# Modulation on VectorE, and the two halves of the square sums joined on GpSimd, in an 8-core encoder step

## The chip, the cores and the metric

The kernel runs on the 8 cores of one Trainium2 chip. The metric is the device time of the slowest core in microseconds (us), and smaller is better. Most executions of one kernel agree within 0.3%. In some executions the cores of one die (cores 0 to 3, or 4 to 7), in one execution of the kernel before those of both (0.851 to 0.898, 3065.08 us), show a lower granted TensorE clock, and the time is some per cent longer or more. Such executions are on record for 11 of the 20 kernels here, the kernel before among them; what brings them on is not shown. They are called slow here, and no conclusion rests on them.

TensorE is PE in the profile, its weight load PEld, VectorE DVE, ScalarE ACT, GpSimd POOL, SyncE SP. "L655" is line 655 of the kernel in question; line numbers differ between the kernels, because each has its own text. One helper line issues every matmul, so that line alone does not tell one matmul from another; tile names and shapes do.

## The reference, cut to what matters

There are four layers, prompts of 4 x 4096 rows and 16 sample streams of 16 rows. Every layer has two RMSNorms, each with shift, scale and gate from a conditioning vector `c`.

```python
D_MODEL, SEQ, DEPTH = 1024, 4096, 4

def rms_norm(x, g):
    xf = x.astype(jnp.float32)
    y = xf * lax.rsqrt(jnp.mean(xf * xf, axis=-1, keepdims=True) + EPS)
    return (y * g.astype(jnp.float32)).astype(x.dtype)

def trunk_layer(x, c, hist, pos0, ...):                   # cut
    mod = jnp.dot(jax.nn.silu(c), w_ada) + b_ada          # (B, 6*D): six vectors per sequence
    sh_m, sc_m, gt_m, sh_f, sc_f, gt_f = [m[:, None, :] for m in jnp.split(mod, N_MOD, axis=-1)]
    h = rms_norm(x, g_mix) * (1 + sc_m) + sh_m
    z = jnp.dot(h, w_in)
    p = z[..., :POOL_WIDTH]
    u = jax.nn.gelu(z[..., POOL_WIDTH:POOL_WIDTH + GMLP_WIDTH])
    v = layer_norm(jax.nn.gelu(z[..., POOL_WIDTH + GMLP_WIDTH:]), ln_g, ln_b)
    ...                                                   # pooling mixer, spatial gating: cut
    x = x + gt_m * mix
    h = rms_norm(x, g_ffn) * (1 + sc_f) + sh_f
    f = jnp.dot(jax.nn.silu(jnp.dot(h, w_gate)) * jnp.dot(h, w_up), w_down)
    x = x + gt_f * f
    return x, new_hist, v
```

## The kernel before

The kernel is a Python program that lists some thousands of operations, orders them with a list scheduler of its own, and then emits one instruction stream per engine. The scheduler places each operation by a cost that is written beside it, in us. An operation may name two engines (`flex`: VectorE or ScalarE), and then the scheduler chooses. Two programs are made: even cores take the first half of a prompt and 64 sample rows, odd cores the second half. Each core picks its program at run time (the "role branch").

The activations lie transposed in SBUF: 128 partitions times 8 blocks (`KC`) make the 1024 features, and rows run along the free dimension. The mean of squares over the features is then a sum over partitions, which a matmul with a constant matrix `meanb` (every element 1/1024) does. For 256 rows:

```python
def stats(src, n, Rsrc, rs, ro, Rrs, lead, add=ADD):      # ADD = 4
    kk, bk = (4 if n > 128 or add < ADD else KC), bank()
    for k0 in range(0, KC, kk):                           # two halves of four blocks each
        q, ks = r_sq.new(), kk // add
        p = r_sp.new() if add > 1 else q
        ...
        flex(... out=sv(), in0=src[:, k0:k0+kk, :], in1=src[:, k0:k0+kk, :], op=ALU.mult), 0.065 + kk*n/960,
             ... activation(out=sv(), in_=src[:, k0:k0+kk, :], func=AF.Square), 0.067 + kk*n/1200, ...)
        m = kk
        while m > ks:                                     # 4 blocks -> 2 -> 1, the last one in bf16
            m //= 2
            dve(... out=pv() if m == ks else sv(0, m), in0=sv(0, m), in1=sv(m, 2*m), op=ALU.add), ...)
        pe(mms(None, lambda ...: [(B(bk)[:, 0:n], meanb[:, :], pv()[:, k, :],
                                   k0 + k == 0, k0 + kk == KC and k == ks - 1) for k in range(ks)]), ...)
    act(... AF.Ln ...)                                    # Ln, then Exp with scale -0.5: the rsqrt
    act(... AF.Exp, scale=-0.5 ...)
```

So each half of the features has its own averaging matmul, and the two accumulate in one PSUM bank. The modulation is 12 groups per layer, each of 32 matmuls with 1 column (odd cores) or 5 (even cores):

```python
def mods(l, g, w):
    bk, m = bank(), l % 2
    def specs():
        wv = V(w, 128, (4, KC * 128))
        return [(B(bk)[:, NV*c:NV*c + NV], wv[:, c, 128*k:128*k + 128], scT[:, k, 0:NV], k == 0, k == KC - 1)
                for c in range(4) for k in range(KC)]
    pe(mms(None, specs), 32 * 0.026, [Rscb, w.res[0]], [bk.res[0]])
    dve(... tensor_tensor(out=modT[...], in0=B(bk)[...], in1=b_adaT[...], op=ALU.add) ...)
```

The sample rows' p and v projections use 64 of the 128 output rows, and come one after the other:

```python
def rows_(self, i, o, nb, w):                             # cut: nb is 64 for sample rows
    pe(mms(None, lambda: [(B(bk)[0:nb, :], V(h, 128, (KC, N))[:, k, o:o + nb], V(w, 128, (KC, 512))[:, k, :],
                           k == 0, k == KC - 1) for k in range(KC)]), ...)
```

Last, `fills`: where the scheduler expects PE to wait long, it has PE run `meanb` x `meanb` matmuls that nobody reads, meant to keep the clock up; whether they do was not tested. They count as busy in the profile (244 of them on core 7, 18.5 us), although they are waiting.

## Time and profile before

The median of the first 6 runs was 2671.88 us (2669.75 to 3100.27, the longest ones slow). The page of the profiled execution (core 7, its slowest), its busy line and three of its rows of 40 slices (each digit is the busy share in tenths; PEclk is the granted clock):

```profile
PE 2616.3 (98%) x17898; PEld 1569.8 (59%) x17898; DVE 1632.1 (61%) x3073; ACT 946.9 (35%) x1603; POOL 181.0 (7%) x311
...
PE   5999999999999999999999999999999999999997
...
PEclk8999999999999999999999999999999999999999
...
PE 93%; DVE 2%; issue 2%; ACT 1%; DMA 1%; ACTq 0%; POOL 0%; another core or an unknown queue 0%; DVEq 0%; POOLq 0%
```

The last line is the chain of waits that ended last. PE is nearly always busy and makes 93% of that chain; only the first slice and the last have room. VectorE and ScalarE are far from full. Two groups of matmuls are what the change is after (name of the tiles, shapes, count, busy us, mean ns, then the idle time before them and what ended it):

```profile
L647 PE MATMUL bank<-heap,meanb 128*128 128x256 bf16 (+2 forms) x174 | 38.3, 263 | 22.0 <-DVE heap L790 18.9
...
L647 PE MATMUL bank<-scT,heap 128*128 128x1 bf16 x1536 | 45.3, 163 | 8.2 <-ACT heap L1198 8.0
```

The first are averaging matmuls, the second modulation. The mean of 163 ns is a pipelined duration. From start to next start a modulation matmul takes about 26 ns, one of 256 columns 109 ns and one of 512 columns 216 ns. The cores view shows that odd cores are the slowest by about 9 us, and that the clock is nearly full:

```profile
core 0: 2662.1 us, clock 0.995
core 1: 2667.6 us, clock 0.994
...
core 6: 2660.9 us, clock 0.993
core 7: 2670.6 us, clock 0.993
```

The windows view of core 7 says where PE idles (columns: window, its length, then busy time and instructions of PE, PEld, DVE, ACT, POOL, the granted clock, the DMA share and GB/s):

```profile
0.00:67.00 67.00, 39.07 (x469) 31.27 (x470) 24.72 (x54) 25.44 (x41) 16.69 (x31) 0.90 0.99 203
67.00:215.00 148.00, 142.06 (x1308) 101.08 (x1306) 133.92 (x296) 103.74 (x176) 18.34 (x37) 0.97 0.61 123
215.00:1500.00 1285.00, 1284.03 (x8489) 746.16 (x8488) 783.84 (x1448) 424.00 (x720) 65.83 (x136) 1.00 0.30 56
1500.00:2630.00 1130.00, 1126.05 (x7304) 669.89 (x7303) 664.14 (x1222) 370.23 (x623) 69.81 (x103) 1.00 0.25 50
2630.00:2671.00 41.00, 25.10 (x336) 21.42 (x333) 25.49 (x57) 23.52 (x47) 10.29 (x5) 0.88 0.27 101
```

Between 215 and 2630 us, PE idles 0.97 + 3.95 = 4.9 us in all. The rest is the start, where data has to arrive (DMA share 0.99 in the first 67 us), and the tail.

### The profile page before, as it was taken

To read this page: it belongs to the slowest core of one execution; us is meant where nothing else is said; L and a number is where in the kernel's file an instruction comes from. 1 tells how busy PE (TensorE), PEld (TensorE's weight loads), DVE (VectorE), ACT (ScalarE), POOL (GpSimd) and SP (SyncE) were. 2 spreads that over 40 slices of the span, in tenths; PEclk is the share of its full clock that TensorE was granted. 3 is DMA by queue.
4 is the path that set the end of the run, shared out by engine and by line. 5 is a ranking of instruction groups with operands and counts; after the bars stand their busy time and mean duration, and the time that the engine had idled before them with its cause. 6 is when DMAs were issued, how large, how long until landed. Compare 5 with 4: busy or idle time off the path is not lost.

```text
span 2670.6 us, 50192 instructions; the slowest of 8 cores (2657.8 to 2670.6 us)
## 1 busy us (share of the span) xinstructions
PE 2616.3 (98%) x17898; PEld 1569.8 (59%) x17898; DVE 1632.1 (61%) x3073; ACT 946.9 (35%) x1603; POOL 181.0 (7%) x311
## 2 busy tenths in 40 slices
PE   5999999999999999999999999999999999999997
PEld 4666555555567655555556665565555775555645
DVE  3899544444689854444478985444467885444456
ACT  3676211111668621111156761111146672111145
POOL 2101000000001000000001010000000110000022
PEclk8999999999999999999999999999999999999999
DMA  9933543441001344344000144444120122211112
GB/s 203 212 60 60 89 83 64 80 80 32 17 1 37 57 95 80 64 79 95 17 17 4 34 87 77 84 89 77 41 48 1 37 49 53 47 25 28 28 48 81
DMA packets 27827, 164.38 MB, mean 62 GB/s; under 512 B 3100, under 2 KB 4268, under 8 KB 12984
## 3 DMA queue, kind: packets, MB, share of 16 engines
q0 software_dynamic: 23344, 149.19, 29.6%
q1 hardware_dynamic: 3544, 10.30, 1.0%
q8 instruction: 150, 2.46, 0.4%
q10 hardware_dynamic: 688, 1.61, 0.2%
q14 instruction: 101, 0.83, 0.1%
HBM read 293.37 MB, written 8.51 MB: 113 GB/s over the span
## 4 chain that ended last, share of the span: by engine, by line
PE 93%; DVE 2%; issue 2%; ACT 1%; DMA 1%; ACTq 0%; POOL 0%; another core or an unknown queue 0%; DVEq 0%; POOLq 0%
PE bank L647 93%; DMA heap<-w_ada 1%; DVE heap L815 0%; DVE heap L790 0%; ACT heap L823 0%; DVE x_sb L849 0%; DVE heap L820 0%; DVE heap L1022 0%; ACT L797 0%; ACTq L1354 0%; ACT heap L785 0%; DVE heap L1029 0%; POOL rv L930 0%; POOL rv L928 0%; ACT heap L891 0%
## 5 line engine op out<-in xcount | busy, mean ns | idle before, releaser
L647 PE MATMUL bank<-heap 128*128 128x512 bf16 (+5 forms) x15096 | 2521.5, 328 | 9.9 <-DVE heap L1124 2.8
L647 PEld LDWEIGHTS bank<-heap 128*128 128x128 bf16 (+1 forms) x15096 | 1451.1, 98 | 1020.4 <-issue 21.2
L849 DVE SCALAR_TENSOR_TENSOR x_sb<-bank,modT,x_sb 128x512 f32<-128x512 f32 (+4 forms) x1200 | 723.4, 613 | 592.7 <-PE bank L647 587.2
L1122 ACT ACTIVATE heap<-bank 128x512 bf16<-128x512 f32 (+4 forms) x447 | 230.1, 519 | 1319.0 <-PE bank L647 1309.4
L1124 DVE TENSOR_TENSOR heap<-heap,bank 128x512 bf16<-128x512 bf16 (+4 forms) x447 | 262.6, 588 | 303.0 <-PE bank L647 295.6
L823 ACT ACTIVATE heap<-heap,modT,gsc 128x256 bf16<-128x256 f32 (+4 forms) x371 | 196.3, 584 | 56.6 <-DVE heap L815 54.0
L815 DVE TENSOR_TENSOR heap<-x_sb,heap 128x512 f32<-128x512 f32 (+4 forms) x284 | 178.1, 655 | 21.5 <-ACT heap L799 11.3
L790 DVE TENSOR_TENSOR heap<-heap 128x256 bf16<-128x256 f32 (+4 forms) x300 | 159.1, 549 | 19.9 <-ACT heap L785 13.6
L785 ACT ACTIVATE heap<-x_sb 128x1024 f32<-128x1024 f32 (+2 forms) x118 | 122.4, 1044 | 137.4 <-DVE x_sb L849 91.5
L653 ACT ACTIVATE heap<-bank 128x512 bf16<-128x512 f32 (+2 forms) x120 | 68.9, 591 | 41.9 <-PE bank L647 37.2
L820 DVE TENSOR_SCALAR heap<-heap,gsc,modT 128x256 bf16<-128x256 f32 (+4 forms) x205 | 75.6, 395 | 1.4
L797 ACT ACT_TABLE_LOAD x53 | 68.0, 1283 | 20.1 <-PE bank L647 18.8
L928 POOL TENSOR_SCALAR rv<-mv 128x1 f32<-128x1 f32 x68 | 19.4, 286 | 778.9 <-DVE mv L927 777.8
L639 POOL DMA_DIRECT2D heap<-w_ada x47 | 26.1, 556 | 595.2 <-PE bank L647 550.2
L1022 DVE SCALAR_TENSOR_TENSOR heap<-bank,small_sb,bias 128x256 f32<-128x256 f32 (+2 forms) x144 | 60.1, 456 | 4.3 <-PE bank L647 3.5
L647 PE MATMUL bank<-heap,meanb 128*128 128x256 bf16 (+2 forms) x174 | 38.3, 263 | 22.0 <-DVE heap L790 18.9
L1122 ACT ACT_TABLE_LOAD x43 | 55.2, 1283 | 9.3 <-PE bank L647 8.2
L647 PEld LDWEIGHTS bank<-scT,heap 128*128 128x128 bf16 x1536 | 45.3, 96 | 15.3 <-issue 8.5
L647 PE MATMUL bank<-scT,heap 128*128 128x1 bf16 x1536 | 45.3, 163 | 8.2 <-ACT heap L1198 8.0
L891 ACT ACTIVATE heap<-bank 128x256 bf16<-128x256 f32 (+2 forms) x136 | 44.7, 380 | 23.1 <-PE bank L647 18.0
L924 ACT ACTIVATE heap<-bank 128x512 f32<-128x512 f32 x68 | 39.9, 600 | 25.0 <-PE bank L647 22.8
L926 DVE BATCH_NORM_STATS2 bnst<-heap 128x6 f32<-128x512 f32 x68 | 46.1, 682 | 4.0 <-ACT heap L924 4.0
(63 smaller groups left out, 669.6 us busy)
## 6 DMA issues: line engine op xcount, KB each, us to landing
heap<-w_ada POOLq DMA_DIRECT2D x47, 1024.0 KB, 9.3
heap<-w_gate POOLq DMA_DIRECT2D x15, 1024.0 KB, 9.7
heap<-w_up POOLq DMA_DIRECT2D x15, 1024.0 KB, 13.4
heap<-w_down POOLq DMA_DIRECT2D x15, 1024.0 KB, 16.3
heap<-w_in POOLq DMA_DIRECT2D x9, 1024.0 KB, 9.4
heap<-w_out POOLq DMA_DIRECT2D x8, 1024.0 KB, 9.2
y_out<-heap SPq DMA_DIRECT2D x14, 512.0 KB, 2.8
heap<-w_gate POOLq DMA_DIRECT2D x7, 768.0 KB, 6.6
```

The source lines that it names most:

```text
L647: r = e.matmul(s[0], s[1], s[2], start=s[3], stop=s[4], **(s[5] if len(s) > 5 else {}))
L653: lambda e: e.activation(out=out(), in_=in_(), func=AF.Identity), 0.067 + n / 1200,
L785: lambda e, sv=sv, k0=k0: e.activation(out=sv(), in_=src[:, k0:k0 + kk, :], func=AF.Square),
L790: dve(lambda e, sv=sv, pv=pv, m=m, ks=ks: e.tensor_tensor(out=pv() if m == ks else sv(0, m), in0=sv(0, m), in1=sv(m, 2 * m), op=ALU.add), ...
L797: act(lambda e: e.activation(out=rv_(), in_=B(bk)[:, 0:n], func=AF.Ln, bias=eps_t[:, 0:1]), 0.15 + n / 1200, [bk.res[0], Rone], [Rrs], "ln ...
L815: dve(lambda e, tv=tv, k0=k0, a=a, b=b, n=n: e.tensor_tensor(out=tv(), in0=src[:, k0:k0 + 2, a:b], in1=rsv(a, b).unsqueeze(1).broadcast_to ...
L820: flex(lambda e, tv=tv, k=k, k0=k0, a=a, b=b, g_=g_, s_=s_: e.tensor_scalar(out=dv()[:, k, a:b], in0=tv()[:, k - k0, :], scalar1=g_, scala ...
L823: lambda e, tv=tv, k=k, k0=k0, a=a, b=b, g_=g_, s_=s_: e.activation(out=dv()[:, k, a:b], in_=tv()[:, k - k0, :], func=AF.Identity, bias=s_ ...
L849: dve(lambda e, so=so, sn=sn, s=s, xv=xv: e.scalar_tensor_tensor(out=xv, in0=B(bk)[:, so:so + sn], scalar=modT[:, m, base + n, s:s + 1], i ...
L1022: dve(lambda e, bk=bk, hd=hd, tv=tv, h0=h0: e.scalar_tensor_tensor(out=tv()[:, hd - h0, :].rearrange("p (b t) -> p b t", t=nb), in0=B(bk)[ ...
L1122: act(lambda e: e.activation(out=sv(), in_=B(bks[0])[:, 0:N], func=AF.Silu), 0.067 + N / 1200, [bks[0].res[0]], [sg.res[0]], "silu")
L1124: dve(lambda e: e.tensor_tensor(out=V(a, 128, (a.size // NF // 2, NF))[:, c, 0:N], in0=sv(), in1=B(bks[1])[:, 0:N], op=ALU.mult), 0.071 + ...
```

## The change

Its intent is to take matmuls off the engine that bounds the kernel:

1. **Modulation to VectorE** (odd cores, layers 1 to 3, 9 of 12 groups): a multiply with a running sum over 1024 columns instead of 8 matmuls.
2. **Join**: the two halves of the square sums are added on GpSimd, so that one averaging matmul does for both (both kinds of core).
3. **Paired projections** (even cores): the sample rows' p and v matmuls go to the two column halves of the PE array. The update of the sample rows becomes two VectorE operations instead of four short ones.
4. **Layer norm scaling** may run on ScalarE, for one small GpSimd operation more. **ScalarE table loads** (1283 ns each in the trace before) may be issued ahead of a wait, and the scheduler counts on it.
5. **First load**: the first modulation weights are requested before the role branch.
6. **Settings** of the scheduler retuned for the new operations.

Cut to its core (`...` marks cuts):

```diff
@@ constants: even cores, then odd @@
-    0: dict(RES_MIX=48000, ..., RATE_A=0.6, RATE_B=0.5, ..., SCARCE=3, SWITCH=3.0, SLACK=4.0, LEAD_S=22.0, LEAD_H=7.0, ..., ADD=4, ...
+    0: dict(RES_MIX=40000, ..., RATE_A=0.45, RATE_B=0.4, ..., SCARCE=2, SWITCH=8.0, SLACK=1.0, LEAD_S=16.0, LEAD_H=4.0, ..., ADD=8, ...
+            NSQ=3, LATE=100.0, MODV=(), MODP=7, ...
-    1: dict(RES_MIX=40000, ..., RATE_A=0.45, RATE_B=0.3, ..., SWITCH=3.0, ..., LEAD_F=15.0, ADD=4, ...
+    1: dict(RES_MIX=44000, ..., RATE_A=0.6, RATE_B=0.4, ..., SWITCH=6.0, ..., LEAD_F=2.0, ADD=8, ...
+            NSQ=2, LATE=100.0, MODV=(3, 4, 5, 6, 7, 8, 9, 10, 11), MODP=8, ...
@@ scheduler: table loads @@
-                    st += LOAD
+                    o.early = st - T[e] > 0.2 and seen
+                    ...
+                    st = o.start = max(st, T[e] + LOAD)
@@ modulation on VectorE @@
+            def mods_dve(l, g, w, cb):
+                ...
+                        dve(lambda e, c=c, i=i, t=t: e.scalar_tensor_tensor(
+                            out=V(t, 128, (D,)), in0=V(w, 128, (4, KC * 128))[:, c % 4, :], scalar=1.0,
+                            in1=V(cb, 128, (NV, D))[:, i, :], op0=ALU.mult, op1=ALU.mult,
+                            accum_out=av()[:, c % 4, i:i + 1]), 0.2 + D / 960, ..., -G.LATE)
@@ stats: the join @@
+                    if last:
+                        both.append((q, pv))
+                        continue
...
+                if last:
+                    p = r_sp.new()
+                    S.op({"pool": (0.1 + n / 450, 0.25 + n / 450, lambda e: e.tensor_tensor(
+                        out=V(p, 128, (1, n)), in0=both[0][1](), in1=both[1][1](), op=ALU.add))}, ...)
+                    pe(mms(None, lambda: [(B(bk)[:, 0:n], meanb[:, :], V(p, 128, (n,)), True, True)]), mmc(n), ...)
@@ gated_add: sample rows, two operations for four streams @@
+                    dve(... tensor_tensor(out=tv()..., in0=B(bk)[:, np_:sp.N]..., in1=modT[...].broadcast_to(...), op=ALU.mult) ...)
+                    dve(... tensor_tensor(out=xs, in0=xs, in1=tv(), op=ALU.add) ...)
@@ paired projections @@
+                def s_group(self, i, o, nb):
+                    pe(mms(None, lambda: [(B(bk)[j*nb:j*nb + nb, :], V(h, 128, (KC, N))[:, k, o:o + nb],
+                                           V(w[j], 128, (KC, 512))[:, k, :], k == 0, k == KC - 1)
+                                          for k in range(KC) for j in range(2)]), ...)
@@ layer norm scaling @@
-                        dve(lambda e: e.tensor_scalar(out=vv(), in0=gv(), scalar1=mv..., scalar2=rv..., subtract, mult) ...)
+                        pool(lambda e: e.tensor_scalar(out=nmr[...], in0=mv[...], scalar1=rv[...], scalar2=-1.0, mult, mult), 0.28, ...)
+                        flex(... tensor_scalar as above ..., ... activation(AF.Identity, scale=rv[...], bias=nmr[...]) ...)
@@ first load @@
-                    once(w_ada[0, :, 2 * i:2 * i + 2, :]), [], [wst.res[i]], 1.05, lat=12.5)
+                    once(w_ada[0, :, 2 * i:2 * i + 2, :]), [], [wst.res[i]], 1.05, lat=12.5, tag=f"a{i}")
```

## The prediction

> **What bounds the kernel now.** TensorE. The page gives PE 98% busy on core 7 (2616.3 of 2670.6 us), DVE 61%, ACT 35%, POOL 7%; the chain that ended last is 93% PE. The windows view has PE idle only at the start (28 us of the first 67, 5 more to 140, DMA share about 1.0) and after 2637 us. Between 215 and 2630 us PE idles about 5 us in all.
>
> Odd cores (second half of a prompt) need 2667.6 to 2670.6 us, even ones (with sample rows) 2657.8 to 2662.1 (cores view). The slowest core sets the time.
>
> **What matmuls cost.** From start to next start in the timeline: 216 ns for 512 columns, 109 for 256, 56 for 128, about 26 for the modulation's 1 to 5.
>
> **What the change removes from PE**
> - Modulation: 9 of 12 groups move to VectorE for layers 1 to 3, on odd cores only (the even list is empty). 27 groups x 32 matmuls x 26 ns = 22.5 us.
> - Averaging: two matmuls become one. Core 7: 142 wide ones, half go, 71 x 0.11 = 7.8 us, 0.5 from narrow ones. Core 0: 8.4 us.
> - Sample rows' p and v projections (even cores): 64 matmuls of 512 columns that fill 64 of 128 output rows, 14.5 us, become pairs in the two column halves. [...] I count 6 us.
>
> Odd cores lose about 31 us, even ones about 15. **Even cores become the slowest.**
>
> **What it adds, off PE**
> - VectorE, odd: 108 multiply-and-sum operations over 1024 columns. From 480 ns at 256 and 749 at 512 columns for the same operation, an estimate of 1.3 us each, 140 us, at low priority: 61% to about 66%.
> - GpSimd: about 75 adds of 256 f32 columns. From 2366 ns for 1024, an estimate of 0.6 us each, 45 us. [...] The statistic comes 0.8 us later, but is asked for 8 us or more ahead.
>
> **On the critical path.** Nearly all PE savings from 140 us on. In the DMA-bound start, 1 to 2 us become idle. The first modulation weights are issued before the role branch (now at 6 to 11 us): 0 to 4 us sooner. Early table loads may save 1 to 2 us in the tail.
>
> **Predicted.** Even cores: 2662 - 15 + 1.5 - 3 = about 2645 us; odd about 2639; 1.3 us between span and reported time. 2646 us, range 2633 to 2657. Faster by over 2% (below 2618): 3%. Within 2%: 96%. Slower: 1%.
>
> **What would show each step.** Cores view: parities reversed, odd down about 30, even about 15. Groups: modulation matmuls on odd cores 1536 to 672; averaging ones halved; POOL adds near 0.6 us; VectorE up by 140 us on odd cores. Sample projection: two matmuls in about 256 ns, not 432. PE idle between 215 and 2630 us still under 10 us.
>
> **What would make it wrong.** Column halves run one after the other (even cores 6 us longer); PE waits for statistics held up in POOL's queue, or for banks that a 1.3 us VectorE operation delays; retuned schedule constants change the start more than I allow.

2662 - 15 + 1.5 - 3 = 2645.5, "about 2645", and 1.3 us more is the predicted 2646. The 6 us for the pairs are 14.5 us less 32 pairs at an allowed 256 ns (8.2 us); that the two of a pair would run side by side was not shown at that time. The 0.6 us of the GpSimd add rest on the 2366 ns for 1024 columns (L1320 of the kernel before) alone.

## The result, and the profile after

The kernel after needs 2685.53 us, the median of 20 runs (2683.05 to 3185.23); the kernel before, in 40 runs beside it, 2671.73 us (2669.66 to 3110.33). The ratio is 1.0065, with a 95% interval of 1.005 to 1.008: 0.65% slower. Ratios in this document are the mean time of one kernel's fast runs over that of the other kernel's fast runs of the same rounds, so they are not quite the ratio of the medians quoted. All outputs are correct.

Within 2% was right, but the direction was wrong, and the time lies 28.5 us above the upper end of the range. The lines that answer to those of before (this page is of core 1, now the slowest by 0.1 us; the views below are of core 7 again):

```profile
PE 2600.6 (97%) x17022; PEld 1551.6 (58%) x17022; DVE 1751.5 (65%) x3264; ACT 1013.5 (38%) x1719; POOL 276.6 (10%) x450
...
PE   5999999999999999999999999999999999999996
...
PEclk9989999999999999999999999999999999999998
...
PE 88%; DVE 4%; issue 3%; ACT 2%; POOL 1%; DMA 1%; DVEq 0%; ACTq 0%; POOLq 0%; SPq 0%
...
L846 POOL TENSOR_TENSOR heap<-heap 128x256 bf16<-128x256 f32 (+1 forms) x71 | 73.2, 1031 | 729.4 <-DVE heap L835 650.2
L781 DVE SCALAR_TENSOR_TENSOR heap<-heap 128x1024 bf16<-128x1024 bf16 x108 | 131.5, 1219 | 4.8 <-PE bank L655 1.6
...
L655 PE MATMUL bank<-heap,meanb 128*128 128x256 bf16 (+3 forms) x95 | 23.0, 266 | 44.6 <-POOL heap L846 36.0
```

PE has 876 matmuls fewer (17898 - 17022). But PE's share of the chain that ended last fell from 93% to 88%, and work of VectorE, ScalarE and GpSimd came in its place. The averaging matmuls, nearly halved in number (174 to 95), have twice the idle time before them (44.6 us instead of 22.0), and most of it ends with the join on GpSimd. But most of that is a single wait. PE's waits for statistics on core 7 (us in total, times, longest), before and after:

```profile
PE bank L647 <- DVE heap L790: 18.9, 8, 13.2
```

```profile
PE bank L655 <- POOL heap L846: 37.2, 15, 25.3
```

The longest one stands before the very first matmul, and e4 below shows that it costs little. Between 50 and 2640 us the sums are 5.2 us in 5 waits before (L790) and 11.9 us in 14 waits after (L846). A join takes 1031 ns in the mean.

The cores view and the windows, in the same order as before:

```profile
core 0: 2670.0 us, clock 0.994
core 1: 2684.6 us, clock 0.989
...
core 6: 2671.5 us, clock 0.993
core 7: 2684.5 us, clock 0.989
```

```profile
0.00:67.00 67.00, 33.66 (x451) 28.56 (x452) 21.04 (x50) 23.72 (x38) 18.98 (x33) 0.95 0.98 204
67.00:215.00 148.00, 137.13 (x1289) 99.21 (x1287) 126.88 (x272) 110.69 (x185) 32.13 (x60) 0.94 0.62 123
215.00:1500.00 1285.00, 1273.80 (x7916) 732.01 (x7914) 859.74 (x1587) 468.42 (x790) 105.85 (x199) 1.00 0.30 57
1500.00:2630.00 1130.00, 1120.92 (x7020) 663.23 (x7018) 708.51 (x1296) 384.75 (x659) 100.94 (x150) 1.00 0.25 49
2630.00:2685.00 55.00, 31.32 (x354) 25.28 (x352) 35.35 (x63) 25.91 (x52) 17.97 (x9) 0.82 0.25 95
```

PE idle between 215 and 2630 us is now 11.2 + 9.1 = 20.3 us, against 4.9. In the first 215 us PE is busy 170.8 us instead of 181.1.

To see the whole sum, I gave every matmul of core 7 the time to the next start. Up to the usual spacing of its width that is work; the rest is idle time where the trace shows PE idle, and "late" where it shows none. Averaging, modulation and clock-keeping matmuls (`fills`) are counted by themselves:

| core 7, us | before | after | difference |
|---|---|---|---|
| matmuls of the layers | 2523.8 | 2523.8 | 0 |
| modulation | 39.1 | 17.4 | -21.7 |
| averaging | 19.3 | 11.6 | -7.7 |
| idle | 54.3 | 87.7 | +33.4 |
| clock-keeping matmuls, which are waiting too | 18.2 | 23.1 | +4.9 |
| late starts | 16.0 | 21.0 | +5.0 |
| sum | 2670.7 | 2684.6 | +13.9 |

So the removed work was sized well: 29.4 us, predicted 22.5 + 7.8 + 0.5 = 30.8. It is the waiting that grew, by 43.3 us, and the prediction had next to nothing there. By place, with the layers' matmuls as the clock (the first 80 us of them, up to 2490 us, the rest): the start grew from 150 to 165 us, the middle shrank from 2466 to 2456, the tail grew from 54 to 64. Only 10 of the 29 us removed came through in the middle, and start and tail gave back more than that.

On even cores (core 0) the two averaging matmuls gave 8.5 us and the paired projections 7.1, and idle time took 16.8 and late starts 7.2: 2662.1 became 2670.0.

### The profile page after: what moved, and what is told of

It reads as the page before. It is cut to its first block, busy times and chain, and to the rows that moved or that the text cites. A ratio compares the mean times of both kernels' runs of the same rounds, so it can differ in the third digit from the quotient of the medians.

```text
span 2684.6 us, 49353 instructions; the slowest of 8 cores (2664.9 to 2684.6 us)
## 1 busy us (share of the span) xinstructions
PE 2600.6 (97%) x17022; PEld 1551.6 (58%) x17022; DVE 1751.5 (65%) x3264; ACT 1013.5 (38%) x1719; POOL 276.6 (10%) x450
## 4 chain that ended last, share of the span: by engine, by line
PE 88%; DVE 4%; issue 3%; ACT 2%; POOL 1%; DMA 1%; DVEq 0%; ACTq 0%; POOLq 0%; SPq 0%
PE bank L655 88%; DVE heap L835 1%; POOL heap L846 1%; DVE heap L870 1%; DVE x_sb L903 1%; DMA x_sb<-xin 1%; ACT heap L830 0%; DMA rows<-b_s 0%; ACT heap L878 0%; DVE heap L1102 0%; DVE heap L875 0%; DVE heap L828 0%; ACT L852 0%; DVE heap L1109 0%; DVE heap L1412 0%
## 5 line engine op out<-in xcount | busy, mean ns | idle before, releaser
L878 ACT ACTIVATE heap<-heap,modT,gsc 128x256 bf16<-128x256 f32 (+4 forms) x366 | 190.9, 579 | 75.4 <-DVE heap L870 57.3
L835 DVE TENSOR_TENSOR heap<-heap 128x512 f32<-128x512 f32 (+4 forms) x308 | 167.4, 558 | 28.7 <-ACT heap L830 21.2
L846 POOL TENSOR_TENSOR heap<-heap 128x256 bf16<-128x256 f32 (+1 forms) x71 | 73.2, 1031 | 729.4 <-DVE heap L835 650.2
L830 ACT ACTIVATE heap<-x_sb 128x1024 f32<-128x1024 f32 (+2 forms) x103 | 107.9, 1050 | 83.4 <-DVE x_sb L903 71.5
L781 DVE SCALAR_TENSOR_TENSOR heap<-heap 128x1024 bf16<-128x1024 bf16 x108 | 131.5, 1219 | 4.8 <-PE bank L655 1.6
L661 ACT ACTIVATE heap<-bank 128x512 bf16<-128x512 f32 (+2 forms) x131 | 74.5, 591 | 49.9 <-PE bank L655 39.1
L828 DVE TENSOR_TENSOR heap<-x_sb 128x1024 f32<-128x1024 f32 (+3 forms) x50 | 59.4, 1190 | 18.0 <-DMA x_sb<-xin 13.7
L1102 DVE SCALAR_TENSOR_TENSOR heap<-bank,small_sb,bias 128x256 f32<-128x256 f32 (+2 forms) x144 | 63.3, 456 | 4.9 <-PE bank L655 3.4
L655 PE MATMUL bank<-heap,meanb 128*128 128x256 bf16 (+3 forms) x95 | 23.0, 266 | 44.6 <-POOL heap L846 36.0
L1435 ACT ACT_TABLE_LOAD x51 | 65.4, 1283 | 0.9
L852 ACT ACT_TABLE_LOAD x43 | 55.2, 1283 | 11.9 <-PE bank L655 10.8
L1001 DVE BATCH_NORM_STATS2 bnst<-heap 128x6 f32<-128x512 f32 x68 | 45.9, 684 | 16.1 <-ACT heap L999 15.9
L1206 ACT ACT_TABLE_LOAD x39 | 50.0, 1283 | 1.5 <-DVE heap L1208 0.3
```

The costliest lines, as they stand in the source:

```text
L655: r = e.matmul(s[0], s[1], s[2], start=s[3], stop=s[4], **(s[5] if len(s) > 5 else {}))
L661: lambda e: e.activation(out=out(), in_=in_(), func=AF.Identity), 0.067 + n / 1200,
L781: dve(lambda e, c=c, i=i, t=t: e.scalar_tensor_tensor(out=V(t, 128, (D,)), in0=V(w, 128, (4, KC * 128))[:, c % 4, :], scalar=1.0, in1=V(cb ...
L830: lambda e, sv=sv, k0=k0: e.activation(out=sv(), in_=src[:, k0:k0 + kk, :], func=AF.Square),
L835: dve(lambda e, sv=sv, pv=pv, m=m, ks=ks: e.tensor_tensor(out=pv() if m == ks else sv(0, m), in0=sv(0, m), in1=sv(m, 2 * m), op=ALU.add), ...
L846: S.op({"pool": (0.1 + n / 450, 0.25 + n / 450, lambda e: e.tensor_tensor(out=V(p, 128, (1, n)), in0=both[0][1](), in1=both[1][1](), op=AL ...
```

## The experiments

The theories that the experiments were to tell apart:

- **A, the join.** Statistics come later because of the join on GpSimd; PE waits for them.
- **B, modulation.** The 1.2 us operations on VectorE hold up evictions of PSUM banks.
- **C, the start.** The first load before the role branch takes bandwidth from the first `x` columns.
- **D, the settings** and the other parts (layer norm on ScalarE, table loads).
- **E, chance.** The scheduler's order differs in thousands of places after any edit, and the chip likes some orders better.

Here are all 18 runs. "Odd" and "even" are the mean spans of these cores in one fast execution. The "estimate" beside each is what the scheduler in the kernel expects for the whole program from its own cost formulas; it is an estimate of the kernel's and no measurement, and what matters is how far the chip lies above it. "Stages" are start / middle / tail of core 7 as defined above. A dash means too few fast runs for a ratio.

| run | median us | ratio to before | odd (estimate) | even (estimate) | stages |
|---|---|---|---|---|---|
| before | 2671.73 | | 2669.0 (2650.8) | 2660.2 (2633.6) | 150/2466/54 |
| after | 2685.53 | 1.0065 | 2682.8 (2628.2) | 2669.9 (2623.8) | 165/2456/64 |
| e1_join_dve | 2685.98 | 1.0056 | 2670.7 (2628.9) | 2680.5 (2629.3) | 161/2445/66 |
| e2_no_join | 2749.11 | - | 2658.6 (2625.3) | 2682.2 (2633.7) | 157/2448/54 |
| e3_mod_on_pe | 2717.13 | 1.0175 | 2715.0 (2654.5) | 2669.1 (2623.8) | 161/2485/66 |
| e4_late_first_load | 2683.63 | 1.0042 | 2680.7 (2628.2) | 2669.4 | 162/2455/62 |
| e5_old_settings | 2696.80 | 1.0089 | 2673.9 (2623.5) | 2689.7 (2631.6) | 155/2454/63 |
| e6_old_settings_no_join | 2683.65 | 1.0044 | 2666.1 (2628.3) | 2679.6 (2633.2) | 150/2463/52 |
| e7_layernorm_on_vector | 2724.29 | - | 2686.2 (2640.7) | 2677.8 (2628.6) | 164/2468/63 |
| e8_jitter | 2691.28 | - | 2676.0 (2627.1) | 2684.1 (2630.9) | |
| e9_old_rest | 2672.29 | 1.0001 | 2649.9 (2628.3) | 2669.4 (2633.0) | 150/2446/55 |
| e10_old_table_loads | 2689.60 | 1.0066 | 2661.2 (2636.9) | 2678.6 (2634.5) | |
| e11_old_layernorm | 2917.14 | - | 2655.9 (2629.8) | 2688.8 (2635.7) | |
| e12_old_first_load | 3022.48 | - | 2665.7 (2628.3) | 2679.5 | |
| e13_modulation_only | 2667.57 | 0.9979 | 2651.9 (2628.3) | 2661.3 (2633.6) | 150/2446/56 |
| e14_paired_projection_too | 2664.41 | 0.9974 | 2650.3 (2628.3) | 2662.5 (2627.6) | |
| e15_join_on_gpsimd_alone | 2680.44 | 1.0031 | 2676.6 (2630.2) | 2669.7 (2635.6) | 152/2463/64 |
| e17_nudge | 2784.20 | - | 2657.5 (2637.5) | 2677.4 (2635.8) | |
| e18_join_on_vector_alone | 2755.20 | - | 2668.0 (2633.8) | 2661.0 | 152/2447/68 |
| e19_join_on_gpsimd_squares_on_scalar | 2671.55 | 1.0002 | 2667.1 (2625.4) | 2659.0 | 156/2452/60 |

Where a median is far above the others of its kind (e2, e7, e11, e12, e17, e18), slow executions fell into it; the spans are of a fast one. Some slow ones are also in e5 (2 of 5), in e4 (1 of 4) and in e13 (3 of 8; the median of its fast runs is 2665.46 us).

### First round: one part of the change at a time

**e1_join_dve**: the join on VectorE instead of GpSimd.

```diff
-                    S.op({"pool": (0.1 + n / 450, 0.25 + n / 450, lambda e: e.tensor_tensor(
+                    S.op({"dve": (0.065 + n / 960, 0.155 + n / 960, lambda e: e.tensor_tensor(
```

> The changed kernel with the add that joins the two halves issued on VectorE instead of GpSimd; nothing else edited (the kernel's own scheduler reorders what follows from it). Changed kernel: 2685.5 us, odd cores 2679 to 2685, even 2665 to 2673. Theory A (the GpSimd add is what ate the gain: 1.03 us each instead of 0.6, up to 3.4, and the averaging matmul waits for it): odd cores 2655 to 2668, even 2652 to 2662, time 2657 to 2669, PE idle on core 7 down from 88 us to about 65. Rival B (the modulation products on VectorE delay bank releases): time stays within 5 us of 2685. Rival C (the first x columns arrive later, because the modulation weights now compete with them from 2 us on): time falls by less than 6 us.

Measured: 2685.98 us, as slow as the change: by time alone B's forecast was met and A's missed. But inside, odd cores fell by 12.1 us (2682.8 to 2670.7) and even cores rose by 10.6, and the even ones now set the time. For odd cores this speaks for A. The even ones were a surprise that e8 takes up. In e2, e5, e6, e7, e9, e10 and e11, too, they came out above what the theory under test foresaw, in e5 by 26 us.

**e2_no_join**: no join, two averaging matmuls as before; all else as in the change.

```diff
-            ... ADD=8, ...      (both kinds of core)
+            ... ADD=4, ...
```

> The changed kernel with ADD=4 on both kinds of core, as before the change: two averaging matmuls per statistic, no join anywhere. Theory A: PE gets 8 us of matmuls back but loses the waits: odd 2655 to 2668, even 2658 to 2665, time 2657 to 2669, close to e1_join_dve. Rival B and C: time rises by up to 8 us, to 2686 to 2694.

Measured: the fast executions (2684.37 and 2692.54) allow no ratio, but the spans are clear for odd cores: 2658.6 us, 24.2 less than with the join, although PE does 8 us more averaging. For odd cores A holds. The even ones again came out 12 us longer.

**e3_mod_on_pe**: modulation back on PE, all else as in the change.

```diff
-            ... MODV=(3, 4, 5, 6, 7, 8, 9, 10, 11), MODP=8, ...
+            ... MODV=(), MODP=8, ...
```

> The changed kernel with an empty list of groups for VectorE on odd cores: all modulation back on TensorE, join still on GpSimd. Even cores run the same program (2665 to 2673). Theory A: odd cores get 22 us of matmuls back, 2695 to 2708, time the same. Rival B: odd cores become faster or stay, 2665 to 2685.

Measured: 2717.13 us, and odd cores 32.2 us longer. B falls: far from costing time through late evictions, the move is worth at least the 21.7 us of matmuls that it takes away (the 10 us beyond are about the size of chance, see e8).

**e4_late_first_load**: the first modulation weights requested after the role branch, as before.

```diff
-                    once(w_ada[0, :, 2 * i:2 * i + 2, :]), [], [wst.res[i]], 1.05, lat=12.5, tag=f"a{i}")
+                    once(w_ada[0, :, 2 * i:2 * i + 2, :]), [], [wst.res[i]], 1.05, lat=12.5)
```

> The changed kernel with the first modulation weights issued behind the role branch again, as before the change. Everything after the start has the same order. Theory A: between -4 and +2 us, since work on the layer began only 1.7 us (core 7) and 2.4 us (core 0) later than before the change. Rival C: the first averaging matmul comes at 13 to 16 us instead of 25 to 28 us, and time falls by 6 to 12 us.

Measured: 2683.63 us, odd cores 2.1 us shorter. C falls. In the change the first matmul does come late, at 25.3 us instead of 13.2: the first `x` columns on SyncE's queue landed 12.6 us after their issue instead of 7.2 (core 7), with the weights issued right behind them, from 2.1 us on instead of 5.9. That the two share bandwidth is inferred from this. But the first matmul of a layer comes at 47.5 us instead of 45.8 (44.8 in e4), so that wait mostly moved.

### Second round: settings and layer norm

**e5_old_settings**: the change with the settings of the kernel before, where they exist there (`ADD=8` stays).

```diff
-    0: dict(RES_MIX=40000, ..., RATE_A=0.45, RATE_B=0.4, ..., SCARCE=2, SWITCH=8.0, SLACK=1.0, ...
+    0: dict(RES_MIX=48000, ..., RATE_A=0.6, RATE_B=0.5, ..., SCARCE=3, SWITCH=3.0, SLACK=4.0, ...
-    1: dict(RES_MIX=44000, ..., RATE_A=0.6, RATE_B=0.4, ..., SWITCH=6.0, ..., LEAD_F=2.0, ...
+    1: dict(RES_MIX=40000, ..., RATE_A=0.45, RATE_B=0.3, ..., SWITCH=3.0, ..., LEAD_F=15.0, ...
```

> The changed kernel, join on GpSimd kept, with the schedule settings of the kernel before (lead times, priorities, buffer and load order) in place of the retuned ones. Changed kernel: odd 2679 to 2685, even 2665 to 2673. Theory A2 (the retuned settings lay out an order that is tight on the scheduler's own estimates, and the chip's longer GpSimd adds break it; settings with longer leads hold): odd 2655 to 2670, even 2655 to 2664, time 2657 to 2672. Rival A (the join itself costs the odd cores, whatever the order): odd stay at 2675 to 2685.

Measured: odd cores 8.9 us shorter (the start 10 us better), even ones 19.8 us longer, in all 2696.80. The new settings seem to cost odd cores in the start (without a join it is the same: 157 us in e2 with the new ones, 150 in e6 with the old) and to help even ones; e8 shows how far such differences can be trusted. The forecast under A2 (settings with longer leads help both) missed on both kinds of core.

**e6_old_settings_no_join**: e5 without the join.

```diff
-            ... ADD=8, ...      (on e5)
+            ... ADD=4, ...
```

> The settings of the kernel before and no join (ADD=4): of the change there remain modulation on VectorE (odd), paired sample projections (even), LayerNorm scaling on either engine, early table loads, early first load. Theory A2: odd 2646 to 2656 (before 2669, minus 22 of modulation, plus a few at the start), even 2652 to 2658. Rival D (LayerNorm scaling, with one more GpSimd step ahead of it, and early table loads cost the even cores): even 2670 to 2685 as without join under the new settings (2682).

Measured: odd cores 2666.1, even 2679.6. Against e5 the join costs 7.8 us on odd cores here and 10.1 on even ones. Its sign is the same as in e2, its size is not. And in the middle of core 7 the sign is even the other way round (2454 us with the join, 2463 without). And 2666.1 is still far above what the modulation move should leave (2669.0 - 21.7 = 2647.3): something else costs time, too.

**e7_layernorm_on_vector**: the change with the layer norm scaling on VectorE alone.

```diff
-                        pool(lambda e: e.tensor_scalar(out=nmr[0:nb, q:q + 1], ...
-                        flex(lambda e: e.tensor_scalar(...), ..., lambda e: e.activation(... AF.Identity ...), ...
+                        dve(lambda e: e.tensor_scalar(...), 0.195 + 512 / 1920, ...
```

> The changed kernel with the LayerNorm scaling of v on VectorE only, straight from mean and reciprocal deviation, without the extra GpSimd product. Rival D: even 2655 to 2662, odd 2 to 10 us down. Theory A2: both within 6 us of the changed kernel (odd 2684, even 2670), direction open.

Measured: odd 2686.2, even 2677.8: no gain, so in the presence of the join this is not the cause.

**e8_jitter**: the change with one cost in the scheduler nudged, which changes the order everywhere and means nothing by itself.

```diff
-    HOP = 0.13
+    HOP = 0.14
```

> A control for the scheduler's sensitivity: the changed kernel with the scheduler's assumed hop between engines 0.14 us instead of 0.13, which means nothing on the chip but reorders instructions. If differences of a few us between schedules are chance, odd and even cores move by up to 6 us in either direction; if they move under 2 us, differences of 5 us in the other runs may be read.

Measured: odd cores 6.8 us shorter, even ones 14.2 us longer. This is what chance (E) does, and it sets the limit of all single comparisons here: with e17 below, some 8 us on odd cores, 14 on even ones. Part of it is in the plan already: the scheduler's own estimate moved by -1.1 us on odd cores and by +7.1 on even ones. That even cores were longer in e1, e2 and e6 is therefore explained by no part; the kernel after may simply have had a lucky order on even cores, which its tuning picked. I leave that open.

### Third round: what else costs odd cores time

All of these start from e6 (old settings, no join).

**e9_old_rest**: layer norm on VectorE, old table loads, old first load, and the unused conditioning rows not loaded on even cores.

```diff
-                    o.early = st - T[e] > 0.2 and seen
-                    ...
-                    st = o.start = max(st, T[e] + LOAD)
+                    st += LOAD
```
(and the edits of e4 and e7)

> e6 (old settings, no join) with four more parts put back as before the change: table loads planned and issued as before, LayerNorm scaling on VectorE, first modulation weights behind the role branch, no unused conditioning rows on even cores. Of the change remain modulation on VectorE (odd), paired sample projections and two-step sample updates (even). e6: odd 2664.7 to 2668.4, even 2678.4 to 2680.5; the scheduler's own total for this kernel is 2628.3 (odd) and 2633.0 (even), and before the change the chip took 17 to 20 us (odd) and 24 to 28 us (even) more than that total. Theory E (one of the four parts makes the chip fall 15 to 20 us further behind the plan): odd 2646 to 2652, even 2655 to 2662. Rival F (chance: a new order is 10 to 20 us worse than the one that was picked for the chip): odd 2660 to 2670, even 2670 to 2685.

**e10_old_table_loads**: of these, the table loads alone.

```diff
-                            k, se = k + self.c.SWITCH, max(st, t0 + LOAD)
+                            k, se = k + self.c.SWITCH, st + LOAD
```
(and the edit shown at e9)

> e6 with table loads planned and issued as before the change only. The scheduler's total is 2636.9 (odd), 2634.5 (even), and e6 exceeded its total by 37 (odd) and 46 us (even). If the table loads are the part meant by theory E: excess 17 to 25 us, odd 2654 to 2662, even 2655 to 2662. If not: odd 2670 to 2677, even 2677 to 2684.

**e11_old_layernorm**: of these, the layer norm alone (the edit of e7, on e6).

```diff
-                             lambda e: e.activation(out=vv(), in_=gv(), func=AF.Identity, scale=rv[...], bias=nmr[...]), ...
+                        (VectorE alone, as in e7)
```

> e6 with LayerNorm scaling on VectorE only. The scheduler's total is 2629.8 (odd), 2635.7 (even). If this is the part of theory E: odd 2648 to 2655, even 2658 to 2664. If not: odd 2663 to 2670, even 2678 to 2685.

**e12_old_first_load**: of these, the first load alone (the edit of e4, on e6).

```diff
-                    ... 1.05, lat=12.5, tag=f"a{i}")
+                    ... 1.05, lat=12.5)
```

> e6 with the first modulation weights behind the role branch as before the change; the order of everything else is unchanged, the total too. If the early load is part of theory E: both kinds 5 to 12 us down. If not: within 3 us of e6 (odd 2664.7 to 2668.4, even 2678.4 to 2680.5), as e4 was of the changed kernel.

Measured, odd cores: e6 2666.1, e10 2661.2, e11 2655.9, e12 2665.7, e9 2649.9. The first load does nothing. Layer norm on ScalarE and early table loads cost 16.2 us together, and each undone alone gives back 10.2 and 4.9 us. The number of table loads does not explain it: core 7 has 150 in e6 and 148 in e9 (139 before, 167 after), at 1283 ns each. Each of the single steps is about the size of chance, the 16 us are twice that. In e9 the odd cores have the modulation on VectorE and little else of the change, and they are 19.1 us faster than before.

### Fourth round: from the good version, one part added

**e13_modulation_only**: e9 with the even cores' program as before, so only the modulation of odd cores differs from the kernel before.

```diff
@@ on e9: gated_add, the sample projections and the square buffers as in the kernel before @@
-            NSQ=3, ...
+            NSQ=2, ...
```

> e9 with the even cores' code and settings put back entirely: of the change only the modulation on VectorE (odd cores) remains. The scheduler's totals: even 2633.6 (the kernel before has the same), odd 2628.3 (as e9). Odd 2648 to 2652 as in e9, even 2657 to 2662 as before the change; time 2659 to 2664, a ratio of 0.995 to 0.997 to the kernel before.

Measured: 2667.57 us, 0.9979 of before (0.9965 to 0.9992). Odd cores 2651.9 us: -17.1 of the 22.5 predicted. Even cores, as before, set the time.

**e14_paired_projection_too**: e13 and the paired sample projections.

```diff
-                                self.p_group(i, o, nb, b, ... "s" if kind == "s" ...)
-                                self.v_group(i, o, nb, b, kind == "s")
+                                if kind == "s":
+                                    self.s_group(i, o, nb)
```

> e13 with the paired sample projections on even cores. Scheduler's total 2627.6 (even), 6 us less than e13's. Pairing saves 7 us of matmuls (64 at 108 instead of 216 to 227 ns). If its gain holds: even 2650 to 2656, time 2652 to 2658. If chance of the order eats it: even 2658 to 2672. Odd as in e13.

Measured: 2664.41 us, 0.9974 (0.9961 to 0.9987), 7 us faster than the kernel before. It is not told apart from e13, whose fast runs have a median of 2665.46. Pairing itself works: these are core 0's sample projections, before and in e14.

```profile
L647 PE MATMUL bank<-heap 128*64 128x512 bf16 x64 | 14.9, 381 | 0.0
```

```profile
L654 PE MATMUL bank<-heap 128*64 128x512 bf16 x64 | 7.7, 382 | 0.0
```

One matmul takes as long (382 ns), but the two of a pair overlap, so the 64 cost half; a start follows each 108 ns in the mean instead of 216. Yet the even cores' spans did not move (2661.3 to 2662.5). Longer waits of core 0 for the updates of `x`, nearly all of them of sample rows, took 4.6 us of the 7 (engine, line, what it waited for, us in total, times, longest), e13 and then e14:

```profile
PE bank L654 <- DVE x_sb L903: 3.8, 7, 2.0
```

```profile
PE bank L654 <- DVE x_sb L903: 8.4, 10, 3.0
```

**e15_join_on_gpsimd_alone**: odd cores have e13's program with the join on GpSimd.

```diff
-            ... ADD=4, ...      (odd cores)
+            ... ADD=8, ...
```

> Odd cores: e9 with the join on GpSimd (total 2630.2, 2 us over e9's). Theory A (the join falls behind plan by waits on GpSimd): odd 2660 to 2675, averaging waits of PE on the GpSimd add of 8 us or more past 50 us. If the join was only harmful with the other parts: odd 2644 to 2656. Even cores (another question): e9 without paired projections, total 2635.6: 2660 to 2670.

Measured: odd cores 2676.6 us against 2651.9, so the join costs 24.7 us where it was to save 8. This is the cleanest test of A: same settings, the same parts, one addition. (Even cores carry the new sample update and the old projections here, 2669.7 us; they do not bear on this. That update has no run of its own: even cores with it were 8.4 us longer here than in e13, and 6.9 longer in e9 than in e14, which is within chance.)

**e17_nudge**: e9 with `HOP` nudged, as a second look at chance.

```diff
-    HOP = 0.13
+    HOP = 0.14
```

> e9 with the assumed hop between engines 0.14 us instead of 0.13. Scheduler's totals 2637.5 (odd, e9 2628.3) and 2635.8 (even, e9 2633.0). Chip minus total was 21 (odd) and 36 us (even) in e9. If this excess is a property of the parts: odd 2655 to 2662, even 2668 to 2676. If it is chance of the order: outside these.

Measured: odd cores 2657.5 against 2649.9, so +7.6; even ones 2677.4 against 2669.4. The scheduler's estimate had foreseen +9.2 and +2.8, so on odd cores this is the plan's doing and not the chip's, as the forecast for that case said (2655 to 2662). The join's 24.7 us are three times this, and its estimate foresaw 1.9 of them.

**e18_join_on_vector_alone**: as e15, but the join on VectorE, and the even cores of e13.

```diff
-                    S.op({"pool": (0.1 + n / 450, 0.25 + n / 450, lambda e: e.tensor_tensor(
+                    S.op({"dve": (0.065 + n / 960, 0.155 + n / 960, lambda e: e.tensor_tensor(
```

> e13 (modulation on VectorE only; odd 2651.8, total 2628.3) with the join on VectorE on odd cores (total 2633.8). If the loss of e15 (odd 2676.5) came from GpSimd and VectorE excluding each other: chip minus total about 21 to 26 us as in e9 and e13, odd 2654 to 2662. If it came from one more serial step for the statistic, whoever takes it: odd 2668 to 2680. Even cores unchanged, 2657 to 2663.

**e19_join_on_gpsimd_squares_on_scalar**: as e15 (and with the even cores of e13), but the squares of joined statistics on ScalarE alone, to take two-input operations of VectorE out of the join's way.

```diff
-                    flex(fd, 0.065 + kk * n / 960, fa, ca, rr, [q.res[0]], lead)
+                    if last:
+                        act(fa, ca, rr, [q.res[0]], lead=lead)
```

> e13 with the join on GpSimd on odd cores and the squares of joined statistics always on ScalarE, so that the 1.22 us VectorE operation with two SBUF inputs no longer stands before a GpSimd add (total 2625.4). Mean GpSimd add 0.8 to 0.9 us instead of 1.00, none over 2.5 us but those behind other two-input operations. If that exclusion is most of the loss: odd 2648 to 2660. If not: odd 2665 to 2680.

Measured: e18 costs 16.1 us over e13 on odd cores, e19 15.2. The join on GpSimd, by groups of core 7, e15 and then e19:

```profile
L844 POOL TENSOR_TENSOR heap<-heap 128x256 bf16<-128x256 f32 x67 | 67.3, 1005 | 643.2 <-DVE heap L833 505.0 <-ACT heap L953 35.9 <-DVE mv L1000 35.4
```

```profile
L849 POOL TENSOR_TENSOR heap<-heap 128x256 bf16<-128x256 f32 x67 | 54.5, 813 | 668.1 <-DVE heap L838 519.8 <-DVE heap L827 53.4 <-PE bank L654 36.7
```

With the squares off VectorE the same add takes 813 ns in the mean instead of 1005. So VectorE's work is what lengthens it. But by what was written before the runs, this is not most of the loss. e18 was to come to 2654 to 2662 us on odd cores if the exclusion of the two engines was the cause, and to 2668 to 2680 if it was one more step for the statistic, whoever takes it: it measured 2668.0. e19 was to come to 2648 to 2660 if the exclusion was most of the loss, else to 2665 to 2680: it measured 2667.1, although its adds were as short as forecast.

### What lengthens the join: the trace

An excerpt of the timeline of the kernel after, core 7 (start, duration, engine, line, operation, tiles):

```profile
1399.62 1.22 DVE L828 TENSOR_TENSOR heap<-x_sb 128x1024 f32<-128x1024 f32 x1
1399.86 1.57 POOL L846 TENSOR_TENSOR heap<-heap 128x256 bf16<-128x256 f32 x1 [3.36 <-DVE heap L835]
1400.95 1.56 DVE L835 TENSOR_TENSOR heap<-heap 128x512 f32<-128x512 f32 x2
```

The add (POOL) begins while VectorE squares (L828), and ends at 1401.43, 0.59 us after the square does (1399.62 + 1.22 = 1400.84). Meanwhile VectorE's next pair of adds, which take 1.22 us elsewhere in this trace, takes 1.56: the first of the two takes 1027 ns instead of 685 and ends 0.55 us after GpSimd's add. Where VectorE is idle or reads PSUM, the GpSimd add takes 716 to 731 ns (once 760). Behind a square of 1024 columns it takes 1388 to 1577. In the other direction VectorE's add of 512 columns goes from 685 ns to a median of 1025 during a GpSimd add. Operations of VectorE with an input from PSUM keep their durations (L1102, 256 columns: 474 to 491 ns during an add, 458 to 491 otherwise), and so do the layer norm's statistics with one input (L1001: 659 to 694 and 675 to 695). So in this trace GpSimd's add and an operation of VectorE with two inputs from SBUF exclude each other: behind such an operation of 512 or 1024 columns the add ended 0.58 to 0.62 us after it. Two inputs are not needed for it, though: behind VectorE's cast of 2048 columns (L1280, one input) an add took 1598 ns, and the trace of the kernel before had it in view, where two VectorE operations of 128 columns with one tensor input (L1313) took 1842 and 1424 ns beside GpSimd's multiplications in the tail, and 278 to 286 elsewhere. And it can be worse than one operation:

```profile
2134.30 0.69 DVE L1109 TENSOR_TENSOR heap<-heap 128x512 bf16<-128x512 bf16 x1
2134.54 3.37 POOL L846 TENSOR_TENSOR heap<-heap 128x256 bf16<-128x256 f32 x1 [16.76 <-DVE heap L835]
2134.91 1.22 DVE L828 TENSOR_TENSOR heap<-x_sb 128x1024 f32<-128x1024 f32 x1
2136.04 0.69 DVE L1109 TENSOR_TENSOR heap<-heap 128x512 bf16<-128x512 bf16 x1
2136.64 0.69 DVE L835 TENSOR_TENSOR heap<-heap 128x512 f32<-128x512 f32 x1
...
2138.06 0.27 PE L655 MATMUL bank<-heap,meanb 128*128 128x256 bf16 x1 [2.01 <-POOL heap L846]
```

VectorE's operations overlap each other a little (by 0.09 us each), and the add gets in only when the run ends, at 2137.33, after 2.8 us; it ends 0.58 us later. So a waiting add was not served here between operations of VectorE that follow each other closely: it waited out the end of one and three more in a row, and took 3.37 us where 716 ns is the time of an undisturbed one. PE is idle for 2.01 us until it ends. The prediction had no such term.

### How much of the join's cost is this

PE's waits for the joined statistic between 50 and 2640 us, core 7: e13, whose statistic comes from VectorE's last add (L834), then e15, e18 and e19.

```profile
PE bank L654 <- DVE heap L834: 6.3, 8, 2.3
```

```profile
PE bank L653 <- POOL heap L844: 10.8, 16, 1.8
```

```profile
PE bank L654 <- DVE heap L845: 8.2, 5, 4.7
```

```profile
PE bank L654 <- POOL heap L849: 4.5, 6, 2.2
```

(The last is e19.) By stages (table above), e15 loses 2, 17 and 8 us against e13 in start, middle and tail; e18 loses 2, 1 and 12; e19 6, 6 and 4. So with the join on VectorE the middle is as long as without a join, and with it on GpSimd 16 us longer in e15 and 5 us in e19. The new settings give the same order (2445 in e1, 2456 after), e5 and e6 the opposite one, and the two nudges alone moved the middle by 9 us (e17) and 10 (e8): that GpSimd costs in the middle is likely and not shown. The operations of GpSimd on core 7 exceed the median of their kind in these four runs by 10.2 us in e13, 32.5 in e15, 13.3 in e18 and 15.7 in e19.

Two pairs put a size on the parts. A join on VectorE costs odd cores 12.1 us (e1 against e2) and 16.1 (e18 against e13). Having it on GpSimd instead adds 12.1 (after against e1) and 8.6 (e15 against e18), the same sign twice, each about the size of chance. So half of the loss or more is there without GpSimd.

The named waits for the join explain only 4.5 us of the 17. On core 7 e15 has 7.6 us less of averaging than e13, and 35 us more of waiting: 17.7 idle, 13.3 late starts, 4.2 clock-keeping. Most of the growth in late starts can be named. The trace records the granted clock in pieces, and on core 7 it is at half for 32.0 us in e13 and for 57.3 in e15 (36.4 before, 57.4 after); the layers' matmuls that start in these pieces are late by 4.6 us in e13 and 13.8 in e15. One piece follows the 3.37 us add shown above: from 2139 to 2146 us the mean clock reads 0.51, and eight matmuls of 256 columns take 1.86 us there, 1.03 just before. If the wait is what lowered the clock, it is paid for a second time here; that was not tested. The idle time itself lies in many small pieces, which I could not put down to single causes.

One rival was not run. With the join, both square buffers that odd cores have (`NSQ=2`) are held until the add has ended. Squares waited 12.0 us for that in e15, and 12.7 us for VectorE's last add in e13, so the sum did not grow, but a third buffer was not tried on odd cores.

The tail is longer with a join wherever it is done: 60 to 68 us in the nine kernels with a join whose stages are listed, 52 to 56 in the five without (before, e2, e6, e9, e13). The six other runs fit (cut about 2 us later than the table's): e8, with a join, 63 us, and the five without 51 to 53. This is the most regular trace that the join leaves. In the tail GpSimd also multiplies output rows, and there the exclusion shows at its longest. From the kernel after:

```profile
2658.86 5.09 POOL L1412 TENSOR_TENSOR heap<-heap 128x1024 f32<-128x1024 f32 x2 [1.29 <-ACT heap L854]
...
2659.02 5.48 DVE L1412 TENSOR_TENSOR heap<-heap 128x512 f32<-128x512 f32 x2 [1.47 <-ACT heap L854]
...
2665.90 2.40 PE L655 MATMUL bank<-heap 128*128 128x128 bf16 x21 [5.67 <-DVE heap L1208]
```

VectorE's two multiplications of 512 columns (685 ns is usual for a two-input operation of this size) take 5.48 us beside GpSimd's of 1024; an operation that would free PE stands behind them in VectorE's queue, and PE idles 5.67 us. In e18 two small adds of VectorE (256 columns) took 4.27 us the same way. The kernel before has such a collision in its tail, too, with a wait of 2.8 us. Why the tail is longer with a join is not settled.

## Why the prediction was wrong

**Right.** PE bounds the kernel, and the removed matmuls were sized well: modulation 21.7 us (predicted 22.5), averaging 7.7 (8.3) on core 7, 8.5 (8.4) on core 0, the pairs 7.1 (6). The pairs run fully side by side, one in 216 ns where I allowed 256. That they would was my estimate; the trace of the kernel after shows it (core 0: the two of a pair start 2 to 5 ns apart, the next pair 211 ns or more later). The operation on VectorE was predicted at 1.3 us and 140 us in all, and took 1.22 and 131.5.

**Wrong: "an estimate of 0.6 us each, 45 us" and "The statistic comes 0.8 us later, but is asked for 8 us or more ahead."** This is the step that failed. The join was to be free, and it is not: in e15 it costs odd cores 24.7 us and in e2 its removal gains 24.2 (7.8 in e6), where I had put down 8 us of gain. The lead of 8 us is one that the scheduler asks for, not one that the chip has: before the change PE already waited for statistics five times (L790, 5.2 us between 50 and 2640 us), so some had no slack to spend. The size of the add was wrong as well: 1.03 us in the mean and up to 3.37, 73.2 us in all, because VectorE and GpSimd exclude each other (716 ns alone, 1388 to 1577 behind a square). But that is at most half of the loss: on VectorE the join still costs 16.1 us (e18) and 12.1 (e1). By what path so much is lost is shown only in part, as said above.

**Wrong: "Nearly all PE savings from 140 us on."** For the modulation this held roughly: 17.1 of 22.5 us in e13, 19.1 in e9 (which has other parts too). For the averaging it did not hold at all, and for the pairs not either: e14 removes 7 us of matmuls from even cores and their span stays. So a matmul removed from a busy PE was not always time gained here: in e14 longer waits for the updates of `x` took 4.6 us of the 7.

**Wrong: "0 to 4 us sooner" for the first load, and "1 to 2 us in the tail" for table loads.** The first load does nothing (2.1 us in e4, 0.4 in e12, within chance). The tail grew by 10 us. Early table loads together with the layer norm on ScalarE cost 16.2 us on odd cores in e9 against e6. I had given these two no cost.

**Wrong: the order of the parities.** Even cores did not become the slowest: even ones rose by 9.7 us and odd ones by 13.8. Even alone, though, with 2669.9 us, they would have kept the time above the range (to 2657). On them it is shown only that the pairs gave no time (e14); what else ate the rest stays open, because a nudge moves them by up to 14 us. "PE idle between 215 and 2630 us still under 10 us" was the test I had named, and it read 20.3.

What I named under "what would make it wrong" was near: "PE waits for statistics held up in POOL's queue". It was the further step itself, and VectorE's operations in its way, rather than the queue. The other two guesses there, halves of columns one after the other and banks delayed by VectorE's long operation, fell (e14, e3); the retuned settings may cost odd cores some us in the start (e5 is 8.9 us shorter with the old ones, which is about the size of chance).

In a chain of three steps, the odd cores' sum is: before to e13, modulation alone, -17.1 us; e13 to e2, the new settings and the other parts, +6.7; e2 to after, the join, +24.2; together +13.8. Each step has an uncertainty of some 8 us from chance (e8, e17), so the first and the third are shown (the third with the smaller 7.8 us of e6 against it), and the second is not.

One warning stood in the kernel itself. Its scheduler expects -22.5 us on odd cores from the modulation alone (2650.8 to 2628.3), and with the join 2630.2 (e15). So even by its own costs, which know no exclusion and put the add at 0.67 us, the join brought nothing.

**Open.** Why even cores span 2659 to 2690 us over these runs; why pairs save matmuls and no time; which orders in the tail collide. For these, an order of operations would have to be held fixed while one part changes, which this scheduler does not do.

## What to carry to other kernels

Before an operation goes to GpSimd, look at what VectorE does at the same moment. Here, where both read two operands from SBUF, they took turns: GpSimd's add took 716 ns alone and 1388 to 1577 behind a square of VectorE, and VectorE's add of 512 columns 685 ns alone and a median of 1025 beside it. Some operations with one operand were held up, too (278 to 286 ns alone, 1424 and 1842 beside GpSimd's multiplications). So neither duration from a quiet stretch was right. Work that is off the bounding engine and that nobody waits for soon (the modulation, asked for a layer later) could be moved here for most of its worth (17.1 of 22.5 us); a step put into the chain that the bounding engine waits for cost time here on either engine (24.7 us on GpSimd, 16.1 on VectorE), although it removed work from the bounding one. And where a scheduler reorders everything after each edit, nudge a meaningless constant first to see how large chance is.
